# Half of a projection's products moved from one phase of the kernel into the phase before it

## The chip, the cores and the metric

The kernel runs on one core of one Trainium2 chip. The metric is the device time of one execution in microseconds, from several runs of the same program. One further execution was profiled: its trace gives each engine's instructions, TensorE's granted clock, and what the DMA engines moved.

## The reference

Two layers of a diffusion trunk run for 512 latent tokens and 128 context tokens, 1024 features, in fp32. Layer 0 has two attention mixers over one input projection; their outputs stand side by side and go through one output projection, whose result is scaled by a gate `g1` and added to the residual:

```
sh1, sc1, g1, sh2, sc2, g2 = modulation(c, mod_w, mod_b)      # silu(c) @ mod_w + mod_b, in six parts of 1024
h = rms_norm(x, norm1) * (1 + sc1) + sh1
q_a, k_a, v_a, q_b, k_b, v_b = attn_project(h, w_in)
o_a = blocked_attention(q_a, k_a + context, ...)               # mixer A: 8 heads of 64, all 512 + 128 keys
o_b = neighbourhood_attention(q_b, k_b, v_b, context, rel_bias) # mixer B: 8 heads of 64, a window and the context
x = x + g1 * (concat(o_a, o_b) @ w_out)
x = x + g2 * squared_relu_mlp(rms_norm(x, norm2) * (1 + sc2) + sh2, w1, w2)
```

Layer 1 has a gated DeltaNet in the place of the attention and is not touched. Since `concat(o_a, o_b) @ w_out` is `o_a @ w_out[:512] + o_b @ w_out[512:]`, mixer A's share can be had as soon as mixer A is done.

## The kernel before

Activations lie with features on the 128 partitions and all 640 tokens on the free axis, in 8 blocks of 128 features (`NK`). Each fp32 factor of a projection is split into a rounded part and a rest (`hi`, `lo`); a product is three matmuls, hi x hi, hi x lo and lo x hi. The tokens are taken in two halves of 320 columns (`TH`), one PSUM bank each. `half_steps` (L239) makes one half-block: one block of 128 output features for one token half, 8 input blocks x 3 matmuls, then an evacuation. `dense_steps` (L262) goes over four output blocks at a time; `fetch` (L252) loads two blocks of weights (1 MB) on SP's queue into one of two raw buffers (`w_raw`, L122) and splits them (`split_w`, L224: a copy on ScalarE, a subtraction on VectorE) into pairs that rotate.

The program has two phases (`net_kernel`, L1552). In the first one the order of the work is made by a planner, which simulates the engines and takes instructions when their inputs are ready, by their place in the program; in the second the order is that of the program. A phase ends when all its work is done.

The first phase: `first_norm` (L310) loads the tokens, makes the first two modulation parts and the first norm while the key and value products of mixer A start. Then come the query projection of mixer A in two column groups (`proj`, L620, called at L750 with banks `pj` and `md`), the rotations and transposes, mixer A itself (`pair_a`, L857), and, listed behind it, the projections of mixer B (`pieces`, L927), which the planner lays between. L938 splits mixer A's outputs into `n.act[0:8]`. Then mixer B: `front` (L956) makes scores and softmax of one head (GpSimd multiplies by the reciprocal sums, L781), `back` (L999) transposes the weights and multiplies by the values, in the order written out at L1021. Three parts of layer 0's modulation, `g1`, `sh2` and `sc2` (parts 2, 3, 4), are made by `mod_steps_pe` (L160), four loads of 1 MB with 64 matmul instructions for each part, as fillers (L954) that `back` pulls at L1018, in the one bank `dn`. At the end `n.prefetch` (L1562) fetches the first two blocks of `w_out0`.

The second phase: GpSimd's queue loads the residual `x0` from the input `xT` (L1575), 8 tiles of 320 KB. The output projection (L1583) makes 8 blocks x 2 halves; `resid` (L409) scales by the gate while it adds to the residual. Blocks 0 to 3 alternate the halves, blocks 4 to 7 have their first halves ahead of their second (`wide`), with the norm of the first half between (`between_o`). The MLP follows. `xd` (L1555) is a buffer in DRAM, written at L1591 and read in layer 1.

## Time and profile before

| | us |
|---|---|
| median of three runs | 1821.94 |
| lowest, highest | 1816.6, 1825.35 |
| the profiled execution | 1826.51 |
| its span, first to last instruction | 1824.7 |

The stages in the profiled execution: loads and first norm to 46 us; projections and mixer A to about 250; mixer B, with the last projections in its beginning, to 345; the second phase from 346, its output projection to about 403. On the page a busy share counts recorded instructions; matmuls are pipelined and their ends are modelled, so a busy TensorE is not TensorE at its peak. PE is TensorE's matmul, PEld its weight load, DVE VectorE, ACT ScalarE, POOL GpSimd, SP SyncE. The idle time before an instruction is put down to what ended it.

### The profile page before, as it was taken

Reading aid. Unit: us, or ns where it says so; the run is one execution under the profiler, and the core shown is the slowest. Engines: PE = TensorE matmul, PEld = TensorE weight load, DVE = VectorE, ACT = ScalarE, POOL = GpSimd, SP = SyncE. Lnnn points to the kernel's source line nnn. Section 1 sums busy time; section 2 is a strip of 40 time slices with the busy share of each in tenths; the row PEclk is TensorE's granted clock in tenths of the full one; section 3 lists DMA queues with packets and bytes.
Section 4 is the critical chain, followed back from the end, with each engine's and each line's share of the span. In section 5 each row is a group of like instructions: output and inputs, shape, how many; then the busy total and the mean of one; then the engine's idle time right before and its main releaser. Section 6 shows DMA issues by size and latency. Waiting matters only on the chain.

```text
span 1824.7 us, 34900 instructions
## 1 busy us (share of the span) xinstructions
PE 1737.5 (95%) x14120; PEld 1629.9 (89%) x14120; DVE 1266.0 (69%) x2554; ACT 920.5 (50%) x2037; POOL 214.0 (12%) x218
## 2 busy tenths in 40 slices
PE   5999998898999999999989999999998999999999
PEld 4898875698999999998888878888998999999999
DVE  6766567479978778787687877777459857465562
ACT  4555575235336172554756656656635417254360
POOL 0233324100000000000232222212100000000000
PEclk9999998999999999999999999999999999999999
DMA  9101058324433436254122212232142313222131
GB/s 347 57 27 50 26 177 267 127 79 153 145 98 128 139 94 200 77 177 155 49 50 70 50 48 72 48 84 73 61 150 93 116 47 97 89 70 93 59 111 51
DMA packets 174994, 187.22 MB, mean 103 GB/s; under 512 B 48457, under 2 KB 152137, under 8 KB 174833
## 3 DMA queue, kind: packets, MB, share of 16 engines
q1 hardware_dynamic: 170272, 175.05, 30.5%
q0 software_dynamic: 1408, 5.41, 0.9%
q10 hardware_dynamic: 3152, 4.52, 0.7%
q8 instruction: 111, 1.82, 0.4%
q14 instruction: 51, 0.41, 0.1%
HBM read 170.97 MB, written 11.37 MB: 100 GB/s over the span
## 4 chain that ended last, share of the span: by engine, by line
PE 61%; DVE 11%; ACT 3%; DMA 2%; issue 2%; POOL 0%; SPq 0%; DVEq 0%; ACTq 0%; POOLq 0%
PE dn L245 7%; PE dn L246 7%; PE dn L247 7%; PE dn L474 7%; PE p L247 5%; PE p L245 5%; PE p L246 5%; PE p L474 4%; PE s L474 4%; DVE ma L192 3%; DMA t<-in_mod_w_dram 2%; DVE t L229 1%; PE p L1438 1%; PE p L1447 1%; PE ob L1440 1%
## 5 line engine op out<-in xcount | busy, mean ns | idle before, releaser
L228 ACT CAST t<-t 128x1024 fp32r<-128x1024 f32 x169 | 176.7, 1048 | 250.0 <-PE p L246 131.7
L229 DVE TENSOR_TENSOR t<-t 128x1024 fp32r<-128x1024 f32 x169 | 207.5, 1230 | 59.8 <-ACT t L228 58.4
L245 PE MATMUL dn<-t 128*128 128x320 f32 x648 | 210.1, 324 | 7.9 <-ACT t L228 4.8
L246 PE MATMUL dn<-t 128*128 128x320 f32 x648 | 210.4, 325 | 0.0
L247 PE MATMUL dn<-t 128*128 128x320 f32 x648 | 209.7, 324 | 0.2 <-DVE t L229 0.2
L246 PE MATMUL p<-hl,t 128*128 128x320 f32 x448 | 138.5, 309 | 0.0
L245 PEld LDWEIGHTS dn<-t 128*128 128x128 f32 x648 | 124.8, 193 | 12.3 <-ACT t L228 5.5
L246 PE MATMUL dn<-hl,t 128*128 128x320 f32 x416 | 129.5, 311 | 0.0
L192 DVE SCALAR_TENSOR_TENSOR ma<-t,ma 128x1024 f32<-128x1024 f32 x98 | 122.5, 1278 | 9.1 <-DMA t<-in_mod_w_dram 9.1
L246 PEld LDWEIGHTS dn<-t 128*128 128x128 f32 x648 | 124.6, 192 | 4.0 <-issue 2.5
L247 PEld LDWEIGHTS dn<-t 128*128 128x128 f32 x648 | 124.5, 192 | 3.8 <-issue 2.5
L413 DVE SCALAR_TENSOR_TENSOR x<-p,t,x 128x192 f32<-128x192 f32 (+2 forms) x154 | 53.1, 384 | 106.1 <-PE p L247 106.1
L245 PE MATMUL p<-hh,t 128*128 128x320 f32 x392 | 121.2, 309 | 0.0
L247 PE MATMUL p<-hh,t 128*128 128x320 f32 x392 | 121.1, 309 | 0.0
L245 PE MATMUL dn<-hh,t 128*128 128x320 f32 x376 | 117.2, 312 | 0.0
L247 PE MATMUL dn<-hh,t 128*128 128x320 f32 x376 | 116.6, 310 | 0.0
L228 ACT CAST wxh<-t 128x1024 fp32r<-128x1024 f32 x49 | 51.3, 1047 | 91.6 <-PE p L246 49.0
L413 DVE SCALAR_TENSOR_TENSOR x<-dn,t,x 128x320 f32<-128x320 f32 (+1 forms) x86 | 44.8, 524 | 60.7 <-PE dn L247 51.0
L246 PEld LDWEIGHTS p<-hl,t 128*128 128x128 f32 x448 | 84.1, 188 | 0.0
L246 PEld LDWEIGHTS dn<-hl,t 128*128 128x128 f32 x416 | 78.5, 189 | 1.0 <-issue 0.8
L781 POOL TENSOR_TENSOR p<-p,smx 128x640 f32<-128x640 f32 (+1 forms) x48 | 63.9, 1340 | 114.4 <-DVE smx L780 99.9
L245 PEld LDWEIGHTS p<-hh,t 128*128 128x128 f32 x392 | 73.6, 188 | 0.8 <-issue 0.8
(599 smaller groups left out, 5200.7 us busy)
## 6 DMA issues: line engine op xcount, KB each, us to landing
t<-in_mlp_w_dram SPq DMA_DIRECT2D x64, 1024.0 KB
t<-in_mod_w_dram SPq DMA_DIRECT2D x40, 1024.0 KB, 6.2
t<-in_w_qkv_dram SPq DMA_DIRECT2D x12, 1024.0 KB
t<-in_w_in_dram SPq DMA_DIRECT2D x9, 1024.0 KB, 5.4
w<-in_mod_w_dram SPq DMA_DIRECT2D x4, 2048.0 KB, 16.2
t<-in_w_out_dram SPq DMA_DIRECT2D x8, 1024.0 KB, 5.6
bias<-in_biasx_dram SPq DMA_DIRECT2D x8, 512.0 KB, 5.8
t<-in_w_z_dram SPq DMA_DIRECT2D x4, 1024.0 KB
```

What stands on the lines that cost most here:

```text
L192: nc.vector.scalar_tensor_tensor(out=acc[v], in0=wt[:, k], scalar=c, in1=acc[v], op0=ALU.mult, op1=ALU.add)
L228: nc.scalar.copy(hi, raw)
L229: nc.vector.tensor_tensor(out=lo, in0=raw, in1=hi.bitcast(F32), op=ALU.subtract)
L245: self.nc.tensor.matmul(ps, lhsT=hi[:, k, :], rhs=xh[:, ts_], start=(k == 0), stop=False)
L246: self.nc.tensor.matmul(ps, lhsT=hi[:, k, :], rhs=xl[:, ts_], start=False, stop=False)
L247: self.nc.tensor.matmul(ps, lhsT=lo[:, k, :], rhs=xh[:, ts_], start=False, stop=(k == NK - 1))
L413: nc.vector.scalar_tensor_tensor(out=xout[:, a:b], in0=ps[:, a - o:b - o], scalar=self.mod_vec(layer, idx, k, v), in1=xin[:, a:b], op0=ALU ...
L474: nc.tensor.matmul(ps, lhsT=l[:, k, :], rhs=r, start=start and k == 0 and i == 0, stop=stop and k == 3 and i == 2, skip_group_check=True)
L781: nc.gpsimd.tensor_tensor(out=pv, in0=pv, in1=sm.unsqueeze(2).broadcast_to([P, nb, w]), op=ALU.mult)
L1438: nc.tensor.matmul(p1s[d][:, 0:128], lhsT=K[:, 0, bs], rhs=S[d], start=True, stop=True)
L1440: nc.tensor.matmul(ob[:, bs], lhsT=qd[:, d, bs], rhs=S[d], start=(st == 0 and d == 0), stop=False, skip_group_check=True)
L1447: nc.tensor.matmul(p1s[d][:, 128:256], lhsT=E[:, d, nb, :], rhs=rs[d], start=True, stop=True)
```

## The change

Mixer A's share (input blocks 0 to 3) of output blocks 0 to 3 of layer 0's output projection is made in the first phase, behind mixer B in the program. ScalarE scales each half-block by the gate from PSUM into a tile, and GpSimd's queue adds the tile to a copy of the residual in `xd` by an accumulating DMA. The copy is made by four DMAs, DRAM to DRAM, at the start of the program on ACT's queue. The gate (modulation part 2) is made in mixer A, behind the second group of the query projection, no longer as a filler of mixer B. The second phase loads tiles 0 to 3 of the residual from `xd`; of blocks 0 to 3 it makes input blocks 4 to 7 only, with weights in pieces of 512 KB (`fetch_half`), of which the first is fetched at the end of the first phase. Blocks 4 to 7 are made as before.

```diff
-    def half_steps(self, tag, hf, hi, lo, xs, evac):
+    def half_steps(self, tag, hf, hi, lo, xs, evac, k0=0):
...
-        for k in range(NK):
-            xh, xl = xs[k]
+        n = hi.shape[1]
+        for k in range(n):
+            xh, xl = xs[k0 + k]
...
+    def fetch_half(self, w, row0, col0, split=None):
+
+        raw = self.w_raw(NK // 2, 256)
+        self.nc.sync.dma_start(out=raw, in_=w[row0:row0 + D // 2, col0:col0 + 256].rearrange("(k p) c -> p k c", p=P))
+        z = (split or self.split_w)(raw, [P, NK // 2, 256])
+        return [[y[:, :, s * P:(s + 1) * P] for y in z] for s in range(2)]
...
                 proj(["pj", "md", "md", "pj", "pj"] if ch == 0 else ["pj"] * NB, 256 + 256 * ch, xs, ev_q)
+                if ch:
+                    for _ in n.mod_steps_pe(0, 2, "md"):
+                        pass
...
-            n.fillers += [n.mod_steps_pe(0, j, "dn") for j in (2, 3, 4)]
+            n.fillers += [n.mod_steps_pe(0, j, "dn") for j in (3, 4)]
...
             n.fill(99)
+            os_ = [n.act[2 * k:2 * k + 2] for k in range(NK)]
+            op = c.enter_context(tc.tile_pool(name="wo", bufs=1))
+
+            def split(raw, shape):
+                z = [op.tile(shape, F32R, tag=nm, name=nm) for nm in ("woh", "wol")]
+                mulsub(*z, raw)
+                return z
+
+            def ev_o(b, hf, ts_, ps):
+                y = op.tile([P, TH], F32, tag="wy", name="wy", bufs=2)
+                for v, i in (((0, slice(0, TH)),), ((0, slice(0, TS - TH)), (1, slice(TS - TH, TH))))[hf]:
+                    nc.scalar.activation(y[:, i], ps[:, i], AF.Copy, scale=n.mod_vec(0, 2, b, v))
+                nc.gpsimd.dma_start(out=xd[b][:, ts_], in_=y, accum_op=ALU.add)
+
+            for b in range(4):
+                if b % 2 == 0:
+                    ws = n.fetch_half(I["w_out0"], 0, b * P, split)
+                for hf in range(2):
+                    for _ in n.half_steps("dn", hf, *ws[b % 2], os_, lambda *a: ev_o(b, *a)):
+                        pass
...
-            os_ = attn_layer(n)
-            n.prefetch(ins["w_out0"], 0, 0)
+            for k in range(4):
+                nc.scalar.dma_start(out=xd[k], in_=ins["xT"][k * P:(k + 1) * P, :])
+            os_ = attn_layer(n, xd)
+            first = n.fetch_half(ins["w_out0"], D // 2, 0)
...
-                nc.gpsimd.dma_start(out=t, in_=ins["xT"][k * P:(k + 1) * P, :])
+                nc.gpsimd.dma_start(out=t, in_=xd[k] if k < 4 else ins["xT"][k * P:(k + 1) * P, :])
...
-            n.dense(ins["w_out0"], 0, 0, D, os_, lambda k, hf, ts_, ps: n.resid(0, 2, k, hf, ps, x0[k], x0[k], True),
-                    tag=("dn", "p1"), wide=(1,), between=between_o)
+            def last_o(k, hf, ts_, ps):
+                n.resid(0, 2, k, hf, ps, x0[k], x0[k], True)
+
+            for b in range(4):
+                if b % 2 == 0:
+                    ws = first if b == 0 else n.fetch_half(ins["w_out0"], D // 2, b * P)
+                for hf in range(2):
+                    for _ in n.half_steps(("dn", "p1")[hf], hf, *ws[b % 2], os_, lambda *a: last_o(b, *a), k0=4):
+                        pass
+            n.dense(ins["w_out0"], 0, D // 2, D // 2, os_, lambda b, *a: last_o(4 + b, *a), tag=("dn", "p1"), wide=(0,), between=between_o)
```

## Rows read from the trace of the kernel before

**Rows 1.** The page, part 1: busy us of each engine, share, instructions

```profile
PE 1737.5 (95%) x14120; PEld 1629.9 (89%) x14120; DVE 1266.0 (69%) x2554; ACT 920.5 (50%) x2037; POOL 214.0 (12%) x218
```

**Rows 2.** Busy time by stretch: length, engines' busy us (instructions), PEclk, DMA share, GB/s

```profile
0.00:46.00 46.00, 25.04 (x345) 21.22 (x345) 27.92 (x69) 21.31 (x37) 0.71 (x6) 0.96 0.99 347
46.00:250.00 204.00, 191.30 (x1366) 177.55 (x1364) 128.00 (x254) 119.98 (x277) 63.88 (x68) 0.98 0.16 49
250.00:346.00 96.00, 82.57 (x630) 56.94 (x628) 61.84 (x117) 54.86 (x147) 27.36 (x25) 0.91 0.59 182
...
300.00:342.00 42.00, 38.76 (x288) 24.27 (x289) 25.13 (x53) 21.20 (x62) 11.74 (x8) 0.96 0.31 107
354.00:366.00 12.00, 12.00 (x84) 12.00 (x83) 4.54 (x8) 3.29 (x5) 0.00 (x0) 1.00 0.79 278
```

**Rows 3.** Waits of TensorE in 238 to 346: us, times, longest

```profile
PE dn L170 <- DMA t<-in_mod_w_dram: 6.4, 3, 3.2
...
PE t L787 <- DVE t L996: 2.3, 1, 2.3
```

**Rows 4.** TensorE in order of time, second phase: start, us, instruction, idle before

```profile
346.05 0.39 PE L245 MATMUL dn<-t 128*128 128x320 f32 x1 [3.07 <-PEq L78]
...
351.18 0.31 PE L245 MATMUL p<-t 128*128 128x320 f32 x1
...
354.70 0.31 PE L245 MATMUL dn<-t 128*128 128x320 f32 x1
```

**Rows 5.** VectorE and ScalarE in order of time, around the change of phase

```profile
344.88 0.23 DVE L996 TENSOR_TENSOR t<-o,t 128x64 fp32r<-128x64 f32 x1 [0.28 <-ACT t L995]
...
352.80 0.55 DVE L413 SCALAR_TENSOR_TENSOR x<-dn,t,x 128x320 f32<-128x320 f32 x1 [6.49 <-DMA x<-in_xT_dram]
...
362.13 1.05 ACT L228 CAST t<-t 128x1024 fp32r<-128x1024 f32 x1 [7.33 <-DMA t<-in_w_out_dram]
```

**Rows 6.** The start: one DMA issue of ACT's queue; GB/s in 40 slices of 0 to 46

```profile
0.83 0.40 ACTq L660 DMA_DIRECT2D rope<-in_rope_dram  x1
...
GB/s 0 48 316 376 218 353 371 417 401 391 374 395 397 385 386 386 386 386 385 367 348 358 375 388 385 376 381 345 356 368 386 386 385 380 357 357 218 270 378 347
```

**Rows 7.** TensorE in order of time in mixer B: modulation slices, their transposes, scores

```profile
294.33 1.07 PE L170 MATMUL dn<-t 128*32 128x256 f32 x16
...
300.42 1.07 PE L170 MATMUL dn<-t 128*32 128x256 f32 x16
301.42 0.39 PE L979 MATMUL sc<-t,qs 128*128 128x256 f32 x1
...
323.19 0.44 PE L153 MATMUL dn<-t,modm 128*128 128x128 f32 x2
```

**Rows 8.** Busy time by stretch, as rows 2; and an issue of SP's queue

```profile
82.00:88.00 6.00, 3.12 (x26) 2.67 (x25) 4.85 (x9) 4.40 (x10) 2.04 (x2) 0.99 0.35 105
88.00:94.00 6.00, 6.00 (x39) 6.00 (x39) 3.43 (x5) 4.19 (x8) 0.00 (x0) 0.73 0.21 71
...
324.00:330.00 6.00, 3.96 (x20) 2.79 (x22) 3.50 (x10) 2.17 (x9) 1.47 (x1) 0.73 0.01 3
...
30.34 11.00 SPq L609 DMA_DIRECT2D t<-in_w_in_dram  x2
```

**Rows 9.** Lines by their durations, ns min/median/max; groups of the page; DMA issues and landing

```profile
L904 ACT COPY bx<-dn x8: 417/427/435, 149.5 to 231.0; 128x320 f32<-128x320 f32 x8
...
L228 ACT CAST t<-t 128x1024 fp32r<-128x1024 f32 x169 | 176.7, 1048 | 250.0 <-PE p L246 131.7
L229 DVE TENSOR_TENSOR t<-t 128x1024 fp32r<-128x1024 f32 x169 | 207.5, 1230 | 59.8 <-ACT t L228 58.4
...
L1575 POOL DMA_DIRECT2D x<-in_xT_dram x8: 539/539/712, 346.5 to 350.4; - x8
DMA to landing us min/median/max: 6.1/9.1/11.0
...
kk<-kk SPq DMA_DIRECT2D x2, 160.0 KB, 5.9
```

More of the change, by code (lines that the diff above doesn't have):

```diff
@@ L237, in split_act @@
         return hi, lo
-    def half_steps(self, tag, hf, hi, lo, xs, evac):
+    def half_steps(self, tag, hf, hi, lo, xs, evac, k0=0):
         ts_ = slice(hf * TH, (hf + 1) * TH)
         ps = self.bank(tag)[0:hi.shape[2], 0:TH]
-        for k in range(NK):
-            xh, xl = xs[k]
+        n = hi.shape[1]
+        for k in range(n):
+            xh, xl = xs[k0 + k]
             self.nc.tensor.matmul(ps, lhsT=hi[:, k, :], rhs=xh[:, ts_], start=(k == 0), stop=False)
             self.nc.tensor.matmul(ps, lhsT=hi[:, k, :], rhs=xl[:, ts_], start=False, stop=False)
-            self.nc.tensor.matmul(ps, lhsT=lo[:, k, :], rhs=xh[:, ts_], start=False, stop=(k == NK - 1))
-            if k == NK - 1:
+            self.nc.tensor.matmul(ps, lhsT=lo[:, k, :], rhs=xh[:, ts_], start=False, stop=(k == n - 1))
+            if k == n - 1:
                 evac(hf, ts_, ps)
@@ L581, in mlp, with attn_layer @@
                            wide=(1,) if ch == 3 and between else (), between=between if ch == 3 else None)
-def attn_layer(n):
+def attn_layer(n, xd):
     nc, tc = n.nc, n.tc
@@ L1032, in attn_layer @@
             n.fill(99)
-    return [n.act[2 * k:2 * k + 2] for k in range(NK)]
+            os_ = [n.act[2 * k:2 * k + 2] for k in range(NK)]
[15 more added lines that the diff above has]
+                        pass
+    return os_
 def sigmoid(nc, out, x):
```

## The prediction

> **What bounds the kernel now.** First the page: TensorE's matmuls are recorded busy for 1737.5 us of a span of 1824.7, 95% [rows 1]. A change that only moves matmuls gains no more than the idle time it fills, so the question is where TensorE idles. Second the busy time by stage [rows 2]; I cut the span where the work changes. In 0 to 46 us DMA is 0.99 busy and TensorE, busy 25 of 46, waits for inputs. In 46 to 250 (projections, mixer A) TensorE is busy 191.3 of 204 us. In 250 to 346 (mixer B) it is busy 82.57 of 96: 13.4 us are free. In 354 to 366, inside the output projection, both TensorE columns are full. Third, what ends the idle time in mixer B [rows 3]: 6.4 us wait for modulation weights, all before 294 us, and 2.3 for VectorE; 3.07 us more are the change of phase [rows 4]. From 300 to 342 us TensorE is busy 38.76 of 42 [rows 2], so only 3.2 us are free there.
>
> **Output projection, second phase.** Removed there: 4 output blocks x 2 token halves x 4 input blocks x 3 = 96 matmuls of 128x320. From the start at 351.18 to that at 354.70 lie 24 of them [rows 4]: 0.147 us each, 14.1 us in all. They stand on the path, TensorE being full. What could be late next is a weight or a residual tile, because the first four blocks now take 14.1 us, not 28.2. The first residual tile is used at 352.80, 6.75 us after the phase's first matmul [rows 4, 5]; four half-blocks fit in the four banks and last 7.1 us at the full clock, and the first 24 matmuls take 5.1 us instead of 3.5 (346.05 to 351.18), so that is covered. The third fetch (1 MB, for blocks 4 and 5) landed at 362.13 [rows 5], behind 1 MB of weights and beside 2.6 MB of residual; it would be wanted at 346 + 1.6 + 14.1 = 361.7, but half a megabyte less lies ahead of it. I take 0, bound 0 to 2. This term: -14.1 (-14.1 to -12.1).
>
> **The copies at the start.** Four DMAs of 320 KB, DRAM to DRAM, are put on ACT's queue ahead of everything that loads. The table for the rotation, far later in the program, left on that queue at 0.83 us [rows 6], so I expect the copies at once too. From then to 46 us the DMA engines move 340 to 400 GB/s [rows 6] at a busy share of 0.99 [rows 2], and TensorE's work hangs on that stream. 1.31 MB at 385 GB/s is 3.4 us by which everything behind it is late. No row shows a DRAM-to-DRAM copy. The lower bound is 0 (issued later, when DMA is 0.16 busy [rows 2]; nothing needs the copies before mixer B), the upper 6.8, if reading and writing each cost as much as a load. I take 3.4, since a load is the nearest row. The Trainium skill (DMA: Bandwidth & Descriptors, Issuing engines are not separate DMA queues) says that DMAs of all issuing engines share the same 16 DMA engines, which speaks against this part: by it a queue of its own hides nothing, as in the sum; with a free queue the term would be 0 and the sum 3.4 lower.
>
> **The gate, moved into mixer A.** One modulation part is 4 loads of 1 MB, 64 matmul instructions and 2 transposes. 16 instructions take from 300.42 to 301.42, the transposes 0.4 us [rows 7]: 4.4 us leave mixer B and enter the end of mixer A's query projection. There TensorE has one hole: 2.9 us idle in 82 to 88, and the mean granted clock is 0.73 in the 6 us behind it [rows 8], the 1.2 GHz level for about half of them. If the gate's last slices lie in the hole, 1.5 us are added; otherwise 4.4. The loads go through the two raw buffers and SP's queue ahead of mixer B's value weights, which were issued at 40.97 (the second of two, ending at 41.34 [rows 8]) and now wait until the gate's third slice is used; SP's later fetches queue behind. A fetch that comes too late for its matmuls would cost up to 3 us more. I take +2.5, bound 0 to +7.
>
> **Mixer B.** Added: the 14.1 us of matmuls, 12 scalings of 128x320 or less on ScalarE (0.43 us for a whole one), 2 weight splits (1.05 on ScalarE, 1.23 on VectorE each), 8 accumulating DMAs on GpSimd's queue [rows 9]. Removed: the gate's 4.4 us and 4 of 12 loads. Whether the 9.7 us net hide depends on when they can start. They use the single bank that the modulation parts use, and the raw buffers behind the last modulation load. In before the eighth load is used at 294.33 [rows 7]; with eight loads only, the first product weights can be split by about 298. So the 6.4 us of DMA waits are over before the new matmuls may run. They can fill the 3.2 us left in 300 to 342 and regain about 1.4 us of the slow clock in 324 to 330 (0.73 [rows 8]): 4.6 us. 14.1 - 4.4 - 4.6 = +5.1. Bounds: -4.4 (all hidden) to +9.7 (none). ScalarE and GpSimd are 21.2 and 11.7 busy of 42 us [rows 2], so the scalings fit. GpSimd waits for each scaling before it issues its DMA, and the softmax products behind it wait as well, and for those TensorE's transposes; one issue takes 0.54 us [rows 9], 8 of them 4.3 us of an engine with 30 free: nothing.
>
> **The change of phase.** The second phase reads the accumulated rows, so they must have landed. In before mixer B's last work ends at 345.1 and the next phase starts at 346.05 [rows 4, 5]. A load of 320 KB on GpSimd's queue took 6.1 us or more to land, 160 KB between tiles 5.9 [rows 9]. No row shows an accumulating DMA; if the last scaling comes early, nothing is added; if it is the last work, about 6. I take +1.5, because the new work is last in the program but mixer B's tail is a chain of its own; bound 0 to +6.
>
> **Sum.** -14.1 + 0 + 3.4 + 2.5 + 5.1 + 1.5 = -1.6 us. The profiled execution took 1826.5 us (span 1824.7); that is 4.6 above the median of the runs, 1821.94. So 1824.9 against the profile, and 1820.3 against the median, which I predict. What the output projection saves is paid for the most part in stages where TensorE or DMA was full as well.
>
> **Rival 1, hidden (faster).** Matmul records overlap, so "full" may hide room: weight loads are busy only 24.27 of 42 us in 300 to 342, while inside the output projection they fill 12 of 12 [rows 2]. If the difference, 17.7 us, were free, the 9.7 us would vanish and mixer B would even lose 4.4: -14.1 + 3.4 + 2.5 - 4.4 + 1.5 = -11.1, 1811 us. Against it: the modulation slice and the scores behind it start without a gap [rows 7], and mixer B has matmuls of 256 and 512 moving columns, or weights of 32 and 64 columns, which hold the array longer than their weight load does. The Trainium skill reads it as this rival does (Perfetto Trace Analysis, Identifying the Most-Contended Engine: judge TensorE by its weight loads, since matmul busy time misleads); the trace shows that the two columns differ, not that the difference is room. Chance 0.22.
>
> **Rival 2, last in line (slower).** The new products stand behind all of mixer B in the program. If they run mostly after mixer B's own last matmuls, they are a serial tail: mixer B's own work ends at 343 - 4.4 = 338.6; eight half-blocks with one bank cost 12 x 0.147 + 0.43 = 2.2 us each, 17.5; the second weight pair is split only when the first is free, 2.3; then a landing of 6.1 and about 1 us for the change of phase: 365.5, 19.5 us later than 346.05. -14.1 + 3.4 + 2.5 + 19.5 = +11.3, 1833 us. It decides if the first new product starts after about 325. Against it: the planner sets modulation slices between scores that come long before them in the program [rows 7], so it fills gaps early. Chance 0.22.
>
> **How the numbers follow.** The lower bounds together give -18.5, the upper ones +12.6, so no case is sharp. Forecast 0.56, its own range 1812 to 1829; rivals 0.22 each. A measurement of this kernel can tell about 0.5%, 9.1 us, from no change. For 8 in 10 I reach to both rivals, 1809 to 1834. Faster by over 0.5%: rival 1 and a little of the forecast, 0.23; slower: rival 2, 0.22; the same 0.55.
>
> **What would show it.** The first modulation matmuls 3 to 4 us later; the end of mixer A 5 to 6 later; the second phase starting some 12 us later than 346.05; the MLP's first matmul within 3 us of where it was. Wrong if the second phase starts before 350 (rival 1) or after 365 (rival 2), if the start doesn't move (the copies were free), or if TensorE waits for weights inside the output projection.

## The result and the profile after

| | before | after |
|---|---|---|
| median of six runs, us | 1821.99 | 1837.34 |
| lowest, highest | 1816.6, 1825.35 | 1835.97, 1839.46 |
| the profiled execution | 1826.51 | 1837.5 |
| its span | 1824.7 | 1835.4 |

The change made the kernel slower: the ratio is 1.0083, with a 95% interval of 1.0066 to 1.01. The prediction said 1820.3 and a range of 1809 to 1834; both were missed, on the slow side. "Before" stands at 1821.6 to 1822.5 in the comparisons below, and each difference is against the median beside which the kernel was timed.

First the page of the kernel after, its first part (as [rows 1]: busy us of each engine, share of the span, instructions):

```profile
PE 1740.9 (95%) x14120; PEld 1633.4 (89%) x14120; DVE 1268.5 (69%) x2554; ACT 923.1 (50%) x2049; POOL 219.8 (12%) x226
```

As many matmuls as before, 3.4 us more of busy time: nothing was added on TensorE, work was only moved. So most of the 10.7 us between the two spans is idle time of TensorE. The busy time by stretch, cut where the stages now end (columns as in [rows 2]):

```profile
0.00:52.00 52.00, 25.51 (x342) 22.25 (x343) 27.35 (x67) 21.15 (x37) 0.70 (x6) 0.90 0.95 333
52.00:265.00 213.00, 199.53 (x1441) 182.19 (x1440) 130.09 (x257) 120.17 (x280) 63.13 (x66) 0.97 0.21 66
265.00:366.00 101.00, 91.52 (x654) 68.38 (x653) 63.75 (x116) 57.95 (x157) 34.48 (x35) 0.93 0.61 151
376.00:388.00 12.00, 10.62 (x72) 10.16 (x71) 7.81 (x16) 6.14 (x9) 0.00 (x0) 1.00 0.75 252
```

Each stage up to 366 us is longer than in [rows 2], and the stretch inside the output projection, full before, has holes: 10.62 of 12. The start, in order of time: SP's and ACT's issues.

```profile
1.72 10.28 SPq L328 DMA_DIRECT2D x<-in_xT_dram  x8
12.05 1.46 SPq L332 DMA_DIRECT2D w<-in_mod_w_dram  x2
...
0.84 1.22 ACTq L1595 DMA_DIRECT2D xd<-in_xT_dram  x2
2.43 1.15 ACTq L1595 DMA_DIRECT2D xd<-in_xT_dram  x2
```

The eight token loads took SP until 12.0 to issue (6.9 before), and the modulation weights left at 12.05 (8.72 before). Next the gate in mixer A: SP's issues, TensorE's slices of the gate, the first scores of mixer A, and two stretches.

```profile
46.97 46.25 SPq L167 DMA_DIRECT2D t<-in_mod_w_dram  x4
98.44 3.82 SPq L618 DMA_DIRECT2D t<-in_w_in_dram  x2
...
97.31 1.07 PE L170 MATMUL md<-t 128*32 128x256 f32 x16 [1.61 <-DMA t<-in_mod_w_dram]
99.89 1.94 PE L170 MATMUL md<-t 128*32 128x256 f32 x16 [1.52 <-DMA t<-in_mod_w_dram]
...
102.66 1.63 PE L885 MATMUL sc<-kha,qs 128*128 128x320 f32 x6
...
94.00:100.00 6.00, 2.17 (x26) 1.19 (x30) 3.59 (x6) 3.93 (x8) 0.00 (x0) 0.88 0.89 336
100.00:106.00 6.00, 5.50 (x31) 3.87 (x31) 1.55 (x4) 2.37 (x3) 0.00 (x0) 0.50 0.95 312
```

The four gate loads hold SP's queue from 47 to 93, since the two raw buffers come free late; mixer B's value weights leave at 98.44, not at 40.97 (the second issue of the row in [rows 8]; the first, at 30.34, is the second query group's); TensorE is busy 2.17 of 6 us, waits for the gate's loads, and then runs at the 1.2 GHz level (a granted clock of 0.50). In mixer B, the first new product and the accumulating DMAs (their durations in ns, first and last start, and landing in us):

```profile
317.49 0.39 PE L246 MATMUL dn<-t,woh 128*128 128x320 f32 x1
...
L1058 POOL DMA_DIRECT2D xd<-wy x8: 851/868/1047, 322.3 to 354.6; - x8
...
DMA to landing us min/median/max: 3.4/3.5/3.5
```

Last the second phase: TensorE's waits in 366 to 436.5, and four rows in order of time on TensorE, VectorE and ScalarE, which answer to [rows 4, 5].

```profile
PE dn L246 <- ACT t L228: 4.8, 1, 4.8
PE dn L246 <- PEq L78: 3.1, 1, 3.1
PE p L246 <- DVE x L421: 1.4, 1, 1.4
PE s L314 <- DVE acc L307: 1.1, 1, 1.1
PE dn L248 <- DVE t L229: 0.9, 1, 0.9
...
366.12 0.60 PE L246 MATMUL dn<-t 128*128 128x320 f32 x1 [3.11 <-PEq L78]
...
372.68 0.55 DVE L421 SCALAR_TENSOR_TENSOR x<-dn,t,x 128x320 f32<-128x320 f32 x1 [6.32 <-DMA x<-xd]
...
379.10 2.00 ACT L228 CAST t<-t 128x1024 fp32r<-128x1024 f32 x2 [4.77 <-DMA t<-in_w_out_dram]
...
401.75 0.81 PE L314 MATMUL s<-acc,t 128*128 128x320 f32 x2 [1.13 <-DVE acc L307]
```

The phase starts at 366.12 (346.05 before, [rows 4]). The waits of 4.8 (ahead of the MLP) and 3.1 us (the change of phase) were there before; the three others, 3.4 us together, are new. TensorE's order of time, read at the same five points in both traces, gives the account (us; the right column is the sum of the prediction's terms for the place):

| | before | after | difference | predicted |
|---|---|---|---|---|
| to the first transposes of the keys | 60.2 | 66.5 | +6.3 | +3.4 |
| from there to the second phase | 285.8 | 299.6 | +13.8 | +9.1 |
| from there to the first sums of the norm | 45.7 | 35.6 | -10.1 | -14.1 |
| from there to the end of the trace's matmuls | 1428.8 | 1429.5 | +0.7 | 0 |

### The profile page after: what moved, and what is told of

It reads as the page before. It is cut to its first block, busy times and chain, and to the rows that moved or that the text cites. A ratio compares the mean times of both kernels' runs of the same rounds, so it can differ in the third digit from the quotient of the medians.

```text
span 1835.4 us, 34939 instructions
## 1 busy us (share of the span) xinstructions
PE 1740.9 (95%) x14120; PEld 1633.4 (89%) x14120; DVE 1268.5 (69%) x2554; ACT 923.1 (50%) x2049; POOL 219.8 (12%) x226
## 4 chain that ended last, share of the span: by engine, by line
PE 56%; DVE 13%; DMA 5%; ACT 3%; issue 2%; POOL 0%; SPq 0%; DVEq 0%; ACTq 0%; POOLq 0%
PE dn L482 7%; PE dn L246 6%; PE dn L247 6%; PE dn L248 6%; PE p L246 5%; PE p L248 5%; PE p L247 5%; PE p L482 4%; PE s L482 4%; DVE ma L192 3%; DMA t<-in_mod_w_dram 2%; DMA t<-in_mlp_w_dram 2%; DVE t L229 2%; ACT t L228 1%; PE p L1471 1%
## 5 line engine op out<-in xcount | busy, mean ns | idle before, releaser
L246 PE MATMUL dn<-t 128*128 128x320 f32 x680 | 220.4, 324 | 12.8 <-ACT t L228 9.6
L247 PE MATMUL dn<-t 128*128 128x320 f32 x680 | 220.7, 325 | 0.0
L248 PE MATMUL dn<-t 128*128 128x320 f32 x680 | 219.6, 323 | 0.9 <-DVE t L229 0.9
L246 PEld LDWEIGHTS dn<-t 128*128 128x128 f32 x680 | 130.8, 192 | 18.0 <-ACT t L228 10.6
L248 PEld LDWEIGHTS dn<-t 128*128 128x128 f32 x680 | 130.5, 192 | 4.5 <-issue 2.5
L247 PEld LDWEIGHTS dn<-t 128*128 128x128 f32 x680 | 130.7, 192 | 4.0 <-issue 2.5
L247 PE MATMUL dn<-hl,t 128*128 128x320 f32 x432 | 134.1, 310 | 0.0
L247 PE MATMUL p<-hl,t 128*128 128x320 f32 x432 | 133.6, 309 | 0.0
L192 DVE SCALAR_TENSOR_TENSOR ma<-t,ma 128x1024 f32<-128x1024 f32 x98 | 122.6, 1278 | 10.3 <-DMA t<-in_mod_w_dram 10.3
L246 PE MATMUL dn<-hh,t 128*128 128x320 f32 x392 | 121.8, 311 | 0.0
L248 PE MATMUL dn<-hh,t 128*128 128x320 f32 x392 | 121.3, 309 | 0.0
L246 PE MATMUL p<-hh,t 128*128 128x320 f32 x376 | 116.5, 310 | 0.0
L248 PE MATMUL p<-hh,t 128*128 128x320 f32 x376 | 116.3, 309 | 0.0
L482 PE MATMUL s<-t 128*128 128x320 f32 x576 | 92.3, 309 | 0.0
L482 PEld LDWEIGHTS s<-t 128*128 128x128 f32 x576 | 86.5, 188 | 0.0
```

The lines of the kernel that those rows point to most:

```text
L192: nc.vector.scalar_tensor_tensor(out=acc[v], in0=wt[:, k], scalar=c, in1=acc[v], op0=ALU.mult, op1=ALU.add)
L246: self.nc.tensor.matmul(ps, lhsT=hi[:, k, :], rhs=xh[:, ts_], start=(k == 0), stop=False)
L247: self.nc.tensor.matmul(ps, lhsT=hi[:, k, :], rhs=xl[:, ts_], start=False, stop=False)
L248: self.nc.tensor.matmul(ps, lhsT=lo[:, k, :], rhs=xh[:, ts_], start=False, stop=(k == n - 1))
L482: nc.tensor.matmul(ps, lhsT=l[:, k, :], rhs=r, start=start and k == 0 and i == 0, stop=stop and k == 3 and i == 2, skip_group_check=True)
```

## The experiments

Thirteen kernels undo a part of the change, do one alone, or leave a part out. How far one trace may be trusted is seen first. Two pairs of kernels give TensorE the same instructions in the same order up to the second phase; from the keys to there they take 285.8 and 285.2 us (before and e6), and 284.2 and 279.1 (e9 and e12 below). So one trace tells such a stretch to about 5 us, and the verdicts go by the medians.

| kernel | what it is | difference of medians | 95% interval of the ratio |
|---|---|---|---|
| after | all parts | +15.4 | 1.0066 to 1.01 |
| e1_copies_late | after, copies at about 50 us | +9.8 | 1.0035 to 1.0061 |
| e2_gate_in_b | after, gate in mixer B | +13.6 | 1.0064 to 1.0089 |
| e3_before_copies | before, copies at the start | +10.4 | 1.0042 to 1.007 |
| e4_before_gate | before, gate in mixer A | +6.9 | 1.0025 to 1.005 |
| e5_core_alone | after, copies at about 50 us, gate in mixer B | +4.2 | 1.0012 to 1.0031 |
| e6_before_copies_late | before, copies at about 50 us | -0.9 | 0.9982 to 1.0002 |
| e7_eight_copies | before, eight copies at the start | +5.9 | 1.0017 to 1.004 |
| e9_half_out | before, half the products of four blocks left out | -6.1 | 0.9953 to 0.9976 |
| e10_products_first | e5, products ahead of two modulation parts | +4.8 | 1.0018 to 1.004 |
| e11_gate_own_buffers | e4, three gate loads in buffers of their own | +8.1 | 1.0024 to 1.0053 |
| e12_half_out_order | e9, residual behind the weights | -6.5 | 0.9951 to 0.9976 |
| e13_gate_out | before, gate left out | +2.8 | 0.9999 to 1.002 |
| e14_core_order | e5, residual behind the weights | +4.4 | 1.0011 to 1.0033 |

### The copies: e1, e3, e6, e7

e1 takes the four copies of the changed kernel from the start and puts them on SP's queue behind a tiny write that needs the last normed tile:

```diff
-            for k in range(4):
-                nc.scalar.dma_start(out=xd[k], in_=ins["xT"][k * P:(k + 1) * P, :])
...
+        nc.sync.dma_start(out=xd[0:4, 0, 0:8], in_=xs[7][1].bitcast(F32)[0:4, 0:8])
+        for k in range(4):
+            nc.sync.dma_start(out=xd[k], in_=I["xT"][k * P:(k + 1) * P, :])
```

> The changed kernel with its four DRAM-to-DRAM copies of the residual issued on SP's queue behind a small write that needs the first norm's last tile, so after about 55 us, when DMA is nearly idle, and no longer at the start. Theory: the copies at the start cost all of the 6.3 us by which the first products after the first norm came later in the changed kernel (51.16 against 44.86 us), because they stand ahead of the tokens. Then that point returns to 45 to 46 us and the time falls by 5 to 7 us, to 1830 to 1832. Rival: only their bytes cost (3.4 us), the rest is another order of the work; then it falls by 3 to 4 us, to 1833.5, and the point stays near 48. Second rival: what is lost at the start is hidden later anyway; then the time stays at 1837.

e3 puts the four copies, and nothing else, into the kernel before:

```diff
+            for k in range(4):
+                nc.scalar.dma_start(out=xd[k], in_=ins["xT"][k * P:(k + 1) * P, :])
             os_ = attn_layer(n)
```

> The kernel before with the four copies at the start added and nothing else (nothing reads them; the buffer is written again later). Theory: +5 to +7 us, 1827 to 1829, all of it by 51 us of the span. Rival, bytes only: +3.4, 1825.5. Second rival: 0, 1822.

e6 puts them into the kernel before as e1 does (the three added lines above), e7 is e3 with `range(NK)`, eight copies.

> The kernel before with the four copies and nothing else, but issued at about 55 us. Theory one, the copies cost because they stand in the stream of loads that the start waits for: this runs like the kernel before, within 1.5 us of 1822, and the first transposes of the keys start within 1 us of 60.2. Theory two, copies cost wherever they stand, or any edit of the first phase costs some us because the planner lays the whole phase out anew: 3 to 5 us slower, with the second phase starting 3 or more after 346 though the keys' transposes are in time.

> The kernel before with eight copies of 320 KB at the start in place of four. With four the transposes of the keys started 5.9 us late and the time rose by 10.4. If the copies cost by their bytes, read and written each at the loads' 385 GB/s (6.8 us for four), the keys' transposes start 12 to 13.6 us later than 60.2 and the time is 1836 to 1842. If it is a fixed price, of standing ahead of the token loads or of the issue, the keys start 6 to 8 late and the time is 1831 to 1834.

Late copies cost nothing (e6: -0.9), and making them late in the changed kernel gives back 15.4 - 9.8 = 5.6 us (e1); alone at the start they cost 10.4 (e3; 5 to 7 were expected). SP's issues at the start, in order of time: one row of e6, two of e3, two of e7.

```profile
8.06 1.00 SPq L324 DMA_DIRECT2D w<-in_mod_w_dram  x2
```

```profile
1.73 10.17 SPq L320 DMA_DIRECT2D x<-in_xT_dram  x8
11.95 1.45 SPq L324 DMA_DIRECT2D w<-in_mod_w_dram  x2
```

```profile
1.72 12.93 SPq L320 DMA_DIRECT2D x<-in_xT_dram  x8
15.80 1.20 SPq L324 DMA_DIRECT2D w<-in_mod_w_dram  x2
```

Against e6 the modulation weights leave 3.9 us later with four copies and 7.7 with eight; against before, where they leave at 8.72, it is 3.2 and 7.1 (the eleven kernels without copies at the start lie between 8.0 and 9.4). So far the price goes by bytes, counted once (1.31 MB in 3.2 to 3.9 us are 336 to 406 GB/s). What TensorE makes of it does not: the keys' transposes come at 59.3 (e6; 58.4 to 60.4 in all eleven), 66.1 (e3) and 67.1 (e7), 6.8 and 7.8 us later than in e6. In e3 the granted clock from 30 to 40 us is 0.67, in e7 0.83, in e6 0.91; TensorE idles longer ahead of it. The whole price of eight copies, 5.9, is no higher than that of four, 10.4, so neither expectation for e7 holds as a whole: the loads go by bytes, the keys and the time do not. What is shown is that the place of the copies costs, 5.6 in the changed kernel, and their existence doesn't. Why e3 pays more than its start is open. The difference between e3 and e7 lies behind the keys: from there to the second phase e3 takes 289.2 us and e7 284.0 (before 285.8). TensorE's order there is before's in e7 for the first two thirds of the matmuls, and in e3 almost from the first it isn't: the planner has laid the phase out anew. That would explain the difference, but it is no larger than the 5 us by which two traces of one order differ.

### The gate: e2, e4, e11, e13

e4 makes only the gate's move, e2 undoes only that in the changed kernel:

```diff
+                if ch:
+                    for _ in n.mod_steps_pe(0, 2, "md"):
+                        pass
...
-            n.fillers += [n.mod_steps_pe(0, j, "dn") for j in (2, 3, 4)]
+            n.fillers += [n.mod_steps_pe(0, j, "dn") for j in (3, 4)]
```

> The changed kernel with the gate (modulation part 2) made as a filler of mixer B again, as before; the rest of the change stays. Theory: in the changed kernel the gate costs mixer A 8.4 us (the first scores of mixer B moved by 14.7 us, of which 6.3 came from the start): 4.4 us of matmuls, 3.1 us of waiting for its loads, and slow clock. Undone, the first scores of mixer B come 8 us earlier; mixer B gets 4.4 us of matmuls back and the moved products start after twelve loads, not eight, so part of it is lost again: the time falls by 0 to 4 us, to 1833 to 1837. Rival: the move of the gate is neutral, since its 4.4 us of matmuls are on TensorE either way; then first scores come 4.4 us earlier, mixer B is 4.4 longer, and the time stays within 1 us of 1837. Second rival: later products lie in a tail behind mixer B; then slower by 5 or more.

> The kernel before with the gate moved from mixer B into mixer A and nothing else. Theory: mixer A gets 8.4 us longer, mixer B 4.4 shorter: +4, 1826; the first scores of mixer B 8 us later than before, and loads of the gate waited for near 95 us. Rival: a neutral move, +0 within 1.5 us, with the first scores 4.4 us later. Second rival: mixer B gets shorter by more than the matmuls, because its loads are a third fewer: -3 or less.

Undone beside early copies it gives back 1.7 us (e2), beside late ones 9.8 - 4.2 = 5.6 (e1 against e5); alone it costs 6.9 (e4; 4 were expected). Two rows of SP's issues in e4, and the busy time by stretch there (88 to 94, to be held against [rows 8], and mixer B from its first scores to the second phase):

```profile
39.21 45.67 SPq L167 DMA_DIRECT2D t<-in_mod_w_dram  x4
85.37 5.94 SPq L609 DMA_DIRECT2D t<-in_w_in_dram  x2
...
88.00:94.00 6.00, 3.69 (x29) 3.03 (x30) 3.52 (x6) 4.11 (x7) 0.00 (x0) 0.81 0.99 325
...
263.50:351.70 88.20, 70.25 (x500) 48.96 (x498) 56.23 (x108) 45.66 (x130) 25.79 (x24) 0.84 0.50 139
```

The value weights leave 44 us later than in before (85.37 and 40.97), the value products start at 94.3 and not at 88.9, and mixer A's last scores start 3.4 us later. But half of the loss lies elsewhere: mixer B, which has 4.4 us of matmuls less, lasts 88.2 us and not 84.2, with TensorE idle for 18 of them. e11 was to take the queueing away: three of the four gate loads into a pool of their own.

```diff
-            wt = self.w_raw(2, D)
+            wt = own.tile([P, 2, D], F32, tag="gw", name="gw") if own and s < 3 else self.w_raw(2, D)
...
+            gp = c.enter_context(tc.tile_pool(name="gate", bufs=3))
...
-                    for _ in n.mod_steps_pe(0, 2, "md"):
+                    for _ in n.mod_steps_pe(0, 2, "md", gp):
```

> The kernel before with the gate moved into mixer A, as in the run that cost +6.9, but three of the gate's four loads go into buffers of their own, so that the value weights no longer queue behind them for the two raw buffers. If that queueing is the price (value weights issued at 85 in place of 30, mixer B's first value product at 94.3 in place of 88, TensorE half idle in 88 to 94), the value weights are issued by about 42, the value products start at about 88, and the time is 1821 to 1824. Rival: the price is the layout of the planner, or the 4.4 us of matmuls put into a stage that is full: value products in time, but the second phase still starts at about 350 and the time is 1826 or more.

Its SP issues:

```profile
50.40 1.39 SPq L167 DMA_DIRECT2D gw<-in_mod_w_dram  x3
71.14 0.37 SPq L609 DMA_DIRECT2D t<-in_w_in_dram  x1
```

The first value weights still left at 71.14, because the one gate load that stayed in a raw buffer stood ahead of them, and the value products started at 91.3 (the expectation's 30 for the value weights in before is the query group's issue; theirs is 40.97). The queueing was shortened, not removed; the time did not fall. So the run doesn't tell queueing from layout in mixer A. It does repeat the other half: mixer B lasted 89.1 us, TensorE idle for 22.4 of them. e13 measures that half alone. It is the kernel before without the gate's part (a constant 0.5 stands for the gate).

```diff
+        nc.vector.memset(self.modT[0][:, 16:24, :], 0.5)
...
-            n.fillers += [n.mod_steps_pe(0, j, "dn") for j in (2, 3, 4)]
+            n.fillers += [n.mod_steps_pe(0, j, "dn") for j in (3, 4)]
```

> The kernel before with the gate's modulation part left out altogether (a constant stands in its place, so the result lacks it): 4 loads of 1 MB, 64 matmul instructions and 2 transposes fewer in mixer B, nothing put elsewhere. The prediction credited mixer B with 4.4 us for this. If mixer B is bound by TensorE's work, the second phase starts some 4.4 us earlier and the time is 1816 to 1818. If mixer B is bound by its chain of scores, softmax and transposes and by the loads, the part only filled idle time: the time stays within 2 us of 1822, and all of the 6.9 that the move of the gate cost is what it costs in mixer A's stage and what the layout does with it.

Measured: +2.8, a ratio of 0.9999 to 1.002. Leaving 4.4 us of matmuls and 4 MB of loads out of mixer B gains nothing. The busy time from the first scores to the second phase, in the kernel before and in e13, and TensorE's waits there in e13:

```profile
261.80:346.00 84.20, 70.77 (x545) 46.49 (x543) 55.69 (x110) 46.15 (x131) 26.28 (x24) 0.90 0.59 183
```

```profile
262.80:351.00 88.20, 69.99 (x480) 48.13 (x478) 56.39 (x109) 45.61 (x130) 26.25 (x24) 0.85 0.45 127
...
PE dn L171 <- DMA t<-in_mod_w_dram: 7.7, 3, 3.6
...
PE t L788 <- DVE pp L834: 2.1, 1, 2.1
...
PE sc L980 <- ACT p L780: 1.9, 1, 1.9
```

65 recorded matmul instructions fewer, and yet nearly as many busy us, because more of them run at the low clock (mean 0.85 against 0.90); the idle time is 18.2 us against 13.4. The gate had been filler. Without it TensorE waits 4.0 us more for the softmax chain (the last two rows, which before doesn't have), and 7.7 us, not 6.4 [rows 3], for the weights of the other two modulation parts, still the longest wait of the stage. The planner's order is little changed (without the gate's instructions TensorE's is before's up to the first scores and differs in five places behind them), so it is not a likely cause, but it is not ruled out. (This profiled run, 1830.0, was the slowest of twelve; the verdict rests on the median.)

### The half projection: e5, e9, e10, e12, e14

e5 is the changed kernel with e1's and e2's edits together. e9 is e5 without copies and without the products in mixer B, so that input blocks 0 to 3 of output blocks 0 to 3 are left out altogether:

```diff
-            for b in range(4):
-                if b % 2 == 0:
-                    ws = n.fetch_half(I["w_out0"], 0, b * P, split)
-                for hf in range(2):
-                    for _ in n.half_steps("dn", hf, *ws[b % 2], os_, lambda *a: ev_o(b, *a)):
-                        pass
...
-                nc.gpsimd.dma_start(out=t, in_=xd[k] if k < 4 else ins["xT"][k * P:(k + 1) * P, :])
+                nc.gpsimd.dma_start(out=t, in_=ins["xT"][k * P:(k + 1) * P, :])
```

> The changed kernel with two of its parts taken back: the copies leave only at about 55 us, behind the loads of the start, and the gate is again a filler of mixer B. What is left is the half projection under mixer B. If the prices of the parts simply add up as each costs alone (copies +10.4, gate +6.9, whole change +15.4), the rest is worth -1.9 us and this runs at about 1820. If they add up as each gives when it is taken back (5.9 and 2.1), the rest costs +7.4 and this runs at about 1829. The prediction's own terms for it (-14.1 in the second phase, +9.5 in mixer B with the gate back there, +1.5 at the change of phase) give -3.1, 1819.

> Input blocks 0 to 3 of output blocks 0 to 3 of the output projection are left out altogether; no copies, the gate in mixer B, the first phase as before but for a first fetch of half the size. So it measures what the second phase gives back by itself. The prediction's term is -14.1: 1808, with the first matmul of the phase at about 346 and the norm behind it some 31.6 us later (45.7 before). The changed kernel and two variants show 35.7 from the phase's start to the norm, so -10: 1812. If, in addition, everything behind the norm runs about 5 us longer with this layout, as sums of the medians hint, 1817.

e9 gains 6.1 us where the prediction had 14.1; of the three times that the expectation names, 1817 is nearest to the measured 1816.39. Even for nothing, the 96 matmuls were not worth their own time. TensorE's new waits in e9 from its second phase's start at 342.6 to 413, and the busy time of the stretch with the longest of them, behind which the granted clock falls (0.83 on average):

```profile
PE s L314 <- DVE acc L307: 2.7, 1, 2.7
PE dn L248 <- DVE wxl L229: 1.1, 1, 1.1
PE p L246 <- DVE x L421: 0.7, 1, 0.7
...
372.59:382.59 10.00, 7.34 (x38) 6.71 (x37) 6.54 (x11) 2.28 (x5) 0.00 (x0) 0.83 0.30 105
```

The phase takes 35.6 us to the norm, 10.1 less than before and not 14.1: about 4 us went into waits that were not there (4.5 by the first three rows), for the residual sum (a bank is free only when the residual tile is in and added), for split weights of blocks 4 and 5, and for the last sums of the norm on VectorE. From the norm to the MLP, where VectorE is busy 9.6 to 10 of 10 us in both kernels, about 1 us more goes, so that 9.2 are left at 420 us (9.2 in e5 and 9.4 in the changed kernel as well). The trace of e9 then gives back 6.2 of its gain, measured against e6, in the MLP and in layer 1, which no edit touches. The largest piece, 3.1 us, begins with this row:

```profile
1265.07 0.27 PE L1373 MATMUL L<-rp,y 32*32 32x32 f32 x9 [2.05 <-issue]
...
1261.40:1271.40 10.00, 7.91 (x190) 6.76 (x190) 5.42 (x14) 3.35 (x8) 3.20 (x2) 0.83 0.31 108
```

TensorE stood for 2.05 us waiting for nothing that the profile shows, and then lost clock (0.83; 1.00 in e6 at the same instructions). e12 has the same stop, 2.2 us, at the same line; e5 and the changed kernel don't. What it is wasn't tried. In both traces a load of instructions (16 KB, queue q8) starts 0.5 (e9) and 0.3 us (e12) before the stop, and between it and the load before lie 447 and 490 recorded instructions of TensorE, more than between any two in that region of e6 (65 to 427). A late load of instructions would fit, and is not shown. The second phase's 9.2 less the stop's 3.1 is e9's 6.1, but that ties a median to one trace, which gives back 3.1 more elsewhere.

With the products in mixer B (e5, 1826.66; of the expectation's three times, 1829 is nearest) the time is 4.15 + 6.1 = 10.3 us above e9. Two rows of e5, the busy time of mixer B and the start of its second phase, and GpSimd's last accumulating DMA ahead of that:

```profile
258.00:355.40 97.40, 83.37 (x641) 60.02 (x640) 57.32 (x111) 51.47 (x144) 33.21 (x32) 0.92 0.64 177
...
350.92 0.84 POOL L1058 DMA_DIRECT2D xd<-wy  x1 [2.39 <-ACT wy L1057]
...
355.42 0.60 PE L246 MATMUL dn<-t 128*128 128x320 f32 x1 [5.67 <-PEq L78]
```

Up to the second phase mixer B takes 13.2 us more than before's 84.2; TensorE is busy 12.6 us more, and idle for 14.0 us, before for 13.4. Of the idle time 5.67 us are the change of phase, in place of 3.07 [rows 4]: a product is now the last work, its DMA leaves at 350.92, and the second phase starts when it has landed. So 2.0 us of the products hid in mixer B's own idle time (10.3 before, 8.4 now), and the change of phase took 2.6 back. e10 tries whether the place is at fault: the products are fillers right behind the gate, where TensorE waits for modulation weights (`products` is the loop of the changed kernel, moved up and pausing after each output block).

```diff
-            n.fillers += [n.mod_steps_pe(0, j, "dn") for j in (2, 3, 4)]
+            n.fillers += [n.mod_steps_pe(0, 2, "dn"), products(), n.mod_steps_pe(0, 3, "dn"), n.mod_steps_pe(0, 4, "dn")]
...
-                n.fill(2)
+                n.fill(5)
```

> Like the variant with the half projection alone (copies late, gate in mixer B, 1826.66), but the 96 new matmuls are fillers of mixer B placed right behind the gate and ahead of the other two modulation parts, each pull of fillers taking five in place of two. If the half projection costs 12.6 us of mixer B because it comes last, when the waits for modulation weights (6.4 us in the kernel before, all ahead of 294) are over, it now fills those waits: the second phase starts 4 to 7 us earlier than 355.4 and the time is 1820 to 1823. Rival: mixer B has no room wherever the matmuls stand, since the modulation loads that now come later are waited for later: the second phase starts at 354 to 358 and the time stays within 2 us of 1826.7, or rises.

The first product now starts at 278 (in e5 at 321), and nothing is won: 1826.53, mixer B 95.9 us with 12.9 idle, 2.4 of it the change of phase. What the products fill early, the later modulation parts leave open at the end: up to 300 us TensorE is idle for 5.2 us (7.7 in e5), from 330 on, without the change of phase, for 3.8 (none in e5). The rival of that expectation holds: mixer B has no room for the products at either place.

e12 loads residual tiles 4 to 7 on SP's queue behind the weights of blocks 4 and 5 in e9, e14 does the same in e5:

```diff
-            for k in range(NK):
+            def load_x0(k, eng):
...
+            second = n.fetch_half(ins["w_out0"], D // 2, 2 * P)
+            raw = n.w_raw(NK, 256)
+            nc.sync.dma_start(out=raw, in_=ins["w_out0"][:, D // 2:D // 2 + 256].rearrange("(k p) c -> p k c", p=P))
+            for k in range(4, NK):
+                load_x0(k, nc.sync)
...
```

> Like the kernel in which input blocks 0 to 3 of output blocks 0 to 3 are left out (1816.39), so its result leaves out the same products; now residual tiles 4 to 7 are loaded on SP's queue behind the weights of blocks 4 and 5, not on GpSimd's queue beside them. There the second phase took 35.6 us to the norm, 4 more than 14.1 less than 45.7, with waits of 0.7 for the residual, 1.1 for split weights and 2.7 for the norm's sums. If the late weights of blocks 4 and 5 are what eats the gain, those land 3 us earlier, the phase takes 32 to 33.5 us to the norm and the time falls to 1813 to 1815. If VectorE's own work is what is late next, the weights come earlier, the waits move to the sums and the time stays at 1816 to 1817.

> The whole half projection with its cheapest arrangement so far: copies at about 55 us, gate in mixer B, residual tiles 4 to 7 loaded on SP's queue behind the weights of blocks 4 and 5. Without that last step it took 1826.66. If the late weights cost what the traces show (waits of 1.2 and 1.0 us in the second phase, and slow clock behind them), 1824 to 1825.5; if the sums on VectorE take their place, 1826 to 1827. For it to beat the kernel before, mixer B would have to hide at least 3 us more of the new matmuls, which no trace here shows.

In e12 the waits for the residual and for split weights (0.7 and 1.1 in e9) are gone; one wait is left ahead of the norm. Below it stands what VectorE did just before:

```profile
PE s L314 <- DVE acc L307: 2.8, 1, 2.8
...
365.90 0.76 DVE L190 TENSOR_SCALAR ma<-t 128x1024 f32<-128x1024 f32 x1 [3.18 <-DMA t<-in_mod_w_dram]
...
367.63 2.47 DVE L192 SCALAR_TENSOR_TENSOR ma<-t,ma 128x1024 f32<-128x1024 f32 x2
370.03 0.54 DVE L421 SCALAR_TENSOR_TENSOR x<-dn,t,x 128x320 f32<-128x320 f32 x1
...
372.69 0.49 DVE L307 TENSOR_TENSOR acc<-acc,sq 128x320 f32<-128x320 f32 x1 [0.59 <-ACT sq L306]
```

The phase takes 35.7 us to the norm, as in e9, and the time is the same within the intervals (1815.27 and 1816.39). So the sums on VectorE are next in line, about as late as the weights were, as the rival said. They are not late for want of VectorE's time as such: it idled 3.18 us for the weights of a later modulation part, made that part's products from 365.90 to 370.03, and only then the residual sum of block 6, which the norm needs. The program lists that part behind the output projection, so VectorE's order in this phase is not that of the program everywhere. Before has the same products there, from 383.53 to 387.7, without a wait of TensorE. Whether the wait goes without them wasn't tried. In the full kernel (e14) nothing is won either: 1826.52 against 1826.66. No arrangement tried beats the kernel before, and the traces say why: with the products mixer B lasts 12 to 13 us longer than before's 84.2 (15 to 18 longer than the 80.9 and 79.8 of e9 and e12), for what the second phase gives back with 9 to 11.

## Why the prediction was wrong

The medians make a ladder from before to after, each step one part, to be held against the prediction's terms. By the intervals of the table above a step is good to 2 to 4 us either way.

| step | kernels | measured | predicted |
|---|---|---|---|
| products out of the second phase | before to e9 | -6.1 | -14.1 |
| products into mixer B, change of phase | e9 to e5 | +10.3 | +11.0 (9.7 + 4.4 less 4.6, and 1.5) |
| gate into mixer A, out of mixer B | e5 to e1 | +5.6 | -1.9 (2.5 less 4.4) |
| copies at the start | e1 to after | +5.6 | +3.4 |
| sum | | +15.4 | -1.6 |

**Output projection.** The step that failed first: "They stand on the path, TensorE being full." A stretch that is full of matmuls tells nothing of who is next. In before the rest was late by little: taking 14.1 us of matmuls away brought the residual's loads, a weight split and VectorE's sums to the front within one phase. The text named the late weights with "0 to 2"; that bound held for each wait of the changed kernel by itself (1.4, 1.1, 0.9), not for their sum, and it looked at weights and residual only, not at VectorE's sums, which are late even when the weights are not (e12), behind products of a modulation part whose own weights came late. This term is short by 8 in the medians. About 5 of that are seen up to the MLP in every variant; the other 3 are about what e9 lost at the stop in layer 1, which is argued, not shown.

**The gate.** The other large error, 7.5 us. In the two traces of its step (e5, e1) the stretch from the keys to mixer B's first scores grows by 6.0 us, where +2.5 stood, and mixer B gets 2.7 shorter, where 4.4 were credited. In before the 4.4 are worth nothing (e13), since they were filler in a stage that waits for its chain and for the weights of the other parts. The +2.5 in mixer A allowed "up to 3 us" for a fetch that comes too late; the rows show what that fetch does: SP held for 46 us, value weights 44 to 57 us late, and the value products, which had filled TensorE's holes in 88 to 100, gone from there. The prediction had seen the queue and each of its victims and priced them too low. With the products beside it the removal does help mixer B, by 2.7 us in one pair of traces (e5, e1) and 9 in the other (e2, after), as if TensorE were the bound there; that is argued, and the two pairs differ by 6 us, where traces of one order differ by 5. How much of the rest is queueing and how much the planner's layout stays open (e11).

**Mixer B.** The size was nearly right, in part by luck. I let 4.6 us of the products hide in idle time and regained clock, and allowed 1.5 for the change of phase. Of mixer B's own idle time, 10.3 us without the change of phase, the products filled 2.0 in e5 and none in e10 (10.5 left); in the changed kernel 6.5 were left. The clock gave back about as much as was forecast: in e5 the 14.1 us of matmuls added 12.6 us of busy time to before's, at a mean granted clock of 0.92 for 0.90, so about 1.5 us (an estimate from these numbers). But the same TensorE order without products lasts 84.2 us (before) and 84.7 (e6), and nearly the same order 80.9 (e9) and 79.8 (e12, at 0.93 to 0.94), so what hid is not known to better than 4 us. The change of phase took 2.6 when a product came last, and nothing in the changed kernel (3.11), where the last accumulating DMA left at 354.58 and mixer B's own last matmuls ran to 363. By the medians the errors cancel; the step's 10.3 also starts from e9 with its stop of 3.1 us, which e5 doesn't have. From the keys to the second phase e5's trace is 12.3 us longer than e9's.

**The copies.** Right in kind: the bytes, counted once, delay the loads behind them by 3.2 to 3.9 us (3.4 predicted). What was missing is what TensorE does with late inputs: longer idle time, then the low level of the clock, and a start that is 6 to 7 us late. The Trainium skill's sentence on queues (DMA: Bandwidth & Descriptors, Issuing engines are not separate DMA queues) is borne out: copies issued by ACT delayed SP's loads by those 3.2 to 3.9 us.

**The rivals.** Rival 2 named the point 325 for the first product; it came at 317.5, so the tail was not the mechanism of the changed kernel, though its total (1833) was the nearest. In e5 the tail was there with 2.6 us. Rival 1 was the one to be most wrong: it took the gap between TensorE's two columns for room. In mixer B of e5 the weight loads are busy 60.0 of 97.4 us, and still 2.0 us hid. The Trainium skill's rule that rival 1 drew on (Perfetto Trace Analysis, Identifying the Most-Contended Engine) names MFU beside the weight loads; read by the weight loads alone it would have found 37 us of room there. In this kernel's mixer B the measurement speaks against that reading.

**The range.** The upper bounds as they are listed (-12.1, 6.8, 7, 9.7 and 6) add up to +17.4, not to the +12.6 that the prediction gives; 1821.94 + 17.4 is 1839.3, above the measured 1837.34. Of the terms by themselves only the output projection's left its bounds. The gate's and the copies' were mis-sized inside theirs, to the same side.

**The base.** It was not at fault: 1820.3 is counted from a median, and before's median was 1821.99 beside the changed kernel. It bears on traces only. Before's profiled run stands 4.6 us above its median, the changed kernel's at its median (1837.5 and 1837.34), so the two traces differ by 10.7 and the medians by 15.4. That before's trace stood high fits e6, which has the same TensorE order in the first phase and ends 4.4 us earlier, 1.6 of it before the second phase.

**The signs named beforehand.** First matmul 3 to 4 later: 4.4 (14.8 to 19.2). End of mixer A 5 to 6 later: its last scores start 14 later. Second phase some 12 later, wrong if after 365: 366.1. The MLP's first matmul within 3: 10.6 (417.78 to 428.40). TensorE waiting for weights inside the output projection: 0.9 us. Four of the five spoke against the forecast.

## What to carry to other kernels

A stage in which TensorE idles for a chain and for loads is not at once a place where work fits: hold idle time before and after an edit that only removes work there (here 4.4 us of matmuls out, nothing gained), before counting on it. When matmuls leave a full stretch, list all that runs beside them (loads, splits, sums, residual) with its own lateness, and expect the gain to stop at the sum of the small ones. A step that is moved up takes its loads with it, and where buffers and a queue are shared, every later load waits with them.

## What was not expected of the hardware

- An accumulating DMA of 160 KB from GpSimd's queue took 0.87 us to issue (plain loads 0.54, [rows 9]) and landed 3.5 us later, sooner than the plain loads of 320 KB at L1575 in before (6.1 or more) and the 160 KB between tiles (5.9).
- A late load cost more than its lateness where TensorE idled for it and then ran at the 1.2 GHz level: with four copies 3.2 to 3.9 us at the DMA queue became 6 to 7 us at the keys (granted clock 0.67 in 30 to 40 us). With eight copies, at 0.83 there, 7.1 to 7.7 us became 6.8 to 7.8.
- A stop of 2.05 and 2.2 us on TensorE, with no releaser in the profile, appeared at one line of untouched code in the traces of the two kernels that leave the products out; in no other trace does a stop of that kind last longer than 1.3 us.
